# Down projection's tile 6 done whole, one norm beside half a tile, norm factors read in PSUM, weight splits moved

## The chip, the cores and the metric

The kernel runs on one core of a Trainium2 chip. A core has TensorE (PE) for matrix products, VectorE (DVE), ScalarE (ACT) and GpSimd (POOL) for the rest, and SyncE (SP), whose queue here issues the loads and stores. The metric is the device time of one execution in microseconds. Lower is better.

## The reference, cut to what matters

One layer of a hybrid block over 512 tokens of width 1024, in float32: a half-step SwiGLU FFN, a token mixer (gated DeltaNet beside latent attention) and a second half-step FFN. Each of the three works on a modulated RMS norm of x:

```python
def _modulate(x, shift, scale):
    return _rms(x) * (1.0 + scale[:, None, :]) + shift[:, None, :]
h = _modulate(x, sh1, s1)
x = x + 0.5 * g1[:, None, :] * _swiglu(h, ffn1_w_in[l], ffn1_w_out[l])
h = _modulate(x, sh2, s2)
y = _hybrid_mixer(h, ...)          # proj = h @ w_in, ..., mixed @ w_out
x = x + g2[:, None, :] * y
h = _modulate(x, sh3, s3)
x = x + 0.5 * g3[:, None, :] * _swiglu(h, ffn2_w_in[l], ffn2_w_out[l])
```

The norm needs the sum of squares over all 1024 channels of a token, so it can't be finished before the last channel tile of x is.

## The kernel before, in words

The activations lie transposed: x is eight tiles `xT[t]` of 128 channels by 512 tokens. Every float32 product is three matmuls (`mm3`, lines 259 to 261): the high parts `wh` x `xh`, then `wh` x `xl`, then `wl` x `xh`. A weight unit is 128 columns of a weight matrix, up to 8 x 128 x 128; SP loads it raw (`wr`), ACT casts the high part (`wh`, L191), DVE subtracts for the low part (`wl`, L192). Each of `wr`, `wh` and `wl` has four buffers, so a unit's cast waits until PE has read the unit four before it for the last time. `plan_units` fixes the order of the units, `prefetch` and `next_unit` say where in the code each is loaded and split.

FFN1's down projection (`down` with `norm`) makes the eight tiles of x: tiles 0 to 5 in one piece of 512 columns, three weight units each (`KPARTS`: 8, 8 and 6 of the 22 k-steps), then tile 6's first 256 tokens, tile 7's first, tile 7's second and tile 6's second; tile 6's units are loaded and split twice for this. When a tile is finished, DVE adds it to x (`finish`, L652), ACT squares it (L468), and POOL (first half of the tokens) or DVE (the rest) adds the squares into `na` (L470). This lets the norm of the first 256 tokens run beside the two last half tiles. `norm_half` is that norm: two matmuls sum the squares over the channels (`colsum`, L506), DVE takes mean and eps (`ve`, L512), POOL the power -1/2 (`ry`, L177), DVE makes two diagonal matrices of it (`dg`, L426), a matmul with ones spreads them over the partitions (`spread_diag`, L434), ACT copies the result from PSUM (`rb`, L436), and `modulate` makes of each tile of x a scaled one on DVE (`hm`, L452), the high part of h on ACT (`hh`, L454) and the low part on DVE (`hl`, L446). It is a generator: it runs on by a piece wherever `next(na)` stands.

The mixer begins with `latents`: `first_units` multiplies three weight units with the first 256 tokens of h, then with the second 256. It goes k by k over the three units; after places 5, 11 and 15 (`marks`) it runs a piece of the second half's norm, so the column sum L506 stands after six (k, unit) steps and L434 after twelve. Each unit has an accumulator of a pool of three PSUM banks (`acc`), given out in turn; the third unit's is the bank of the down projection's last half tile. `aux` is a pool of five banks for all else. The mixer's end has the same form: `out_half` makes eight half tiles of 256 tokens, twice, with the first half's norm between the tiles of the second, and FFN2 begins with `first_units`. There `prefetch` in `out_half` places the splits of FFN2's first units.

PE's order is held as the code has it (`matmuls_in_order`); ACT and DVE each take their instructions in the order that the scheduler wrote, one after the other.

## Time and profile before

| | |
|---|---|
| median of three runs | 1085.63 us (1085.16, 1085.63, 1088.35) |
| the profiled execution | 1088.02 us, of it 1086.2 us from the first to the last instruction |
| PE busy | 1056.7 us (97%) |
| DVE, ACT, POOL busy | 575.6, 390.6, 43.6 us |
| mean granted clock of PE | 0.991 |

A busy PE is one with a matmul under way; matmuls overlap, so their durations add up to more than the time that they take, and the pace is read from the starts. Idle time of another engine matters only where PE waits for it.

### The profile page before, as it was taken

How to read it: one execution, taken by the hardware profiler on the slowest of the kernel's cores; microseconds unless marked ns; L12 is line 12 of the kernel's file. 1: busy time of each engine (PE TensorE's matmuls, PEld its weight loads, DVE VectorE, ACT ScalarE, POOL GpSimd, SP SyncE). 2: the span in 40 equal slices, each digit the busy share in tenths (PEclk: the TensorE clock that was granted, in tenths of full speed). 3: DMA queues.
4: the chain of work that ended last, by engine and by line, in shares of the span. 5: the costliest groups of instructions: out<-in, count | busy, mean ns of one | idle time of the engine just before them, and what ended most of it. 6: DMA issues, size and time to landing. Idle time of an engine off the chain costs nothing.

```text
span 1086.2 us, 14130 instructions
## 1 busy us (share of the span) xinstructions
PE 1056.7 (97%) x5583; PEld 883.9 (81%) x5583; DVE 575.6 (53%) x1026; ACT 390.6 (36%) x644; POOL 43.6 (4%) x94
## 2 busy tenths in 40 slices
PE   6999999999999999998999999989999999999998
PEld 5788878788887899887887778988888888888887
DVE  4488984333587455469978546674333333322220
ACT  3342222222222345475584544344222222222220
POOL 1000000000000010102000031300000000000000
PEclk8999999999999999999999989999999999999999
DMA  9989973333697345211222001124333333333320
GB/s 275 270 244 297 288 219 97 95 95 92 205 290 239 109 124 165 74 39 46 71 70 72 21 1 39 40 78 118 98 97 97 97 97 97 91 102 111 97 73 30
DMA packets 210576, 132.04 MB, mean 122 GB/s; under 512 B 13633, under 2 KB 194638, under 8 KB 210510
## 3 DMA queue, kind: packets, MB, share of 16 engines
q1 hardware_dynamic: 210510, 131.14, 41.4%
q8 instruction: 44, 0.72, 0.3%
q14 instruction: 22, 0.18, 0.1%
HBM read 128.63 MB, written 2.49 MB: 121 GB/s over the span
## 4 chain that ended last, share of the span: by engine, by line
PE 86%; DVE 8%; DMA 2%; ACT 2%; issue 2%; SPq 1%; POOL 0%; DVEq 0%; POOLq 0%
PE pa L259 25%; PE pa L260 25%; PE pa L261 25%; DVE wl L192 1%; PE pb L407 1%; DMA ar<-in_w_ada 1%; PE pb L259 1%; PE pb L260 1%; PE pb L261 1%; PE pb L1144 1%; PE pb L1545 1%; DVE cv L1088 1%; DVE hl L446 0%; PE pb L1528 0%; POOL ry L177 0%
## 5 line engine op out<-in xcount | busy, mean ns | idle before, releaser
L191 ACT CAST wh<-wr 128x1024 fp32r<-128x1024 f32 (+1 forms) x170 | 173.7, 1023 | 504.4 <-PE pa L260 344.6
L259 PE MATMUL pa<-hh,wh 128*128 128x512 f32 (+1 forms) x885 | 340.0, 384 | 4.8 <-DVE xT L1731 2.7
L260 PE MATMUL pa<-hl,wh 128*128 128x512 f32 (+1 forms) x885 | 336.1, 380 | 0.0
L261 PE MATMUL pa<-hh,wl 128*128 128x512 f32 (+1 forms) x885 | 335.9, 380 | 0.0
L192 DVE TENSOR_TENSOR wl<-wr,wh 128x1024 fp32r<-128x1024 f32 (+1 forms) x170 | 201.6, 1187 | 236.3 <-ACT wh L191 230.8
L259 PEld LDWEIGHTS pa<-hh,wh 128*128 128x128 f32 x885 | 167.4, 189 | 39.5 <-issue 3.1
L261 PEld LDWEIGHTS pa<-hh,wl 128*128 128x128 f32 x885 | 167.4, 189 | 31.4 <-DVE wl L192 0.4
L260 PEld LDWEIGHTS pa<-hl,wh 128*128 128x128 f32 x885 | 167.5, 189 | 29.2 <-DVE hl L446 0.2
L259 PE MATMUL pa<-ah,wh 128*128 128x512 f32 (+1 forms) x418 | 150.1, 359 | 0.0
L261 PE MATMUL pa<-ah,wl 128*128 128x512 f32 (+1 forms) x418 | 148.8, 356 | 0.0
L260 PE MATMUL pa<-al,wh 128*128 128x512 f32 (+1 forms) x418 | 148.6, 356 | 0.0
L259 PEld LDWEIGHTS pa<-ah,wh 128*128 128x128 f32 x418 | 79.0, 189 | 12.6 <-ACT wh L191 1.7
L261 PEld LDWEIGHTS pa<-ah,wl 128*128 128x128 f32 x418 | 79.0, 189 | 11.4
L260 PEld LDWEIGHTS pa<-al,wh 128*128 128x128 f32 x418 | 79.0, 189 | 11.0
L590 DVE TENSOR_TENSOR af<-sg,pa 128x512 f32<-128x512 f32 x40 | 27.5, 687 | 103.3 <-PE pa L261 102.6
L544 DVE SCALAR_TENSOR_TENSOR aa<-ar,sc,aa 128x512 f32<-128x512 f32 x98 | 73.2, 751 | 14.2 <-DMA ar<-in_w_ada 12.5
L652 DVE SCALAR_TENSOR_TENSOR xT<-pa,mod,xT 128x512 f32<-128x512 f32 (+1 forms) x19 | 12.7, 667 | 49.1 <-PE pa L261 49.0
L592 ACT CAST ah<-af 128x512 fp32r<-128x512 f32 x44 | 27.5, 624 | 16.0 <-DVE af L590 16.0
L259 PE MATMUL pa<-mh,wh 128*128 128x256 f32 (+1 forms) x96 | 32.5, 341 | 0.2 <-ACT mh L1572 0.2
L260 PE MATMUL pa<-ml,wh 128*128 128x256 f32 (+1 forms) x96 | 31.3, 326 | 0.0
L261 PE MATMUL pa<-mh,wl 128*128 128x256 f32 (+1 forms) x96 | 31.2, 325 | 0.0
L593 DVE TENSOR_TENSOR al<-af,ah 128x512 fp32r<-128x512 f32 x44 | 30.2, 687 | 0.8 <-ACT ah L592 0.7
(355 smaller groups left out, 1008.8 us busy)
## 6 DMA issues: line engine op xcount, KB each, us to landing
wr<-in_ffn_w_in SPq DMA_DIRECT2D x82, 512.0 KB, 3.9
ar<-in_w_ada SPq DMA_DIRECT2D x48, 512.0 KB, 6.0
wr<-in_ffn_w_out SPq DMA_DIRECT2D x34, 512.0 KB, 4.3
ar<-in_w_ada SPq DMA_DIRECT2D x48, 256.0 KB, 5.1
wr<-in_w_in SPq DMA_DIRECT2D x21, 512.0 KB, 3.9
wr<-in_ffn_w_out SPq DMA_DIRECT2D x17, 384.0 KB, 4.7
wr<-in_w_out SPq DMA_DIRECT2D x8, 512.0 KB, 4.8
wr<-in_ffn_w_in SPq DMA_DIRECT2D x8, 384.0 KB, 7.5
```

Source lines behind the costliest of these rows:

```text
L191: self.nc.scalar.copy(hi, raw)
L192: self.nc.vector.tensor_tensor(out=lo, in0=raw, in1=hi.bitcast(F32), op=ALU.subtract)
L259: mm(out, wh, xh, start=start, stop=False)
L260: mm(out, wh, xl, start=False, stop=False)
L261: mm(out, wl, xh, start=False, stop=stop)
L407: nc.tensor.matmul(pg[32 * q:32 * q + 32, :256], self.sc[:, kc:kc + 1].to_broadcast([P, 32]), a[:, kc], start=(e == 0), stop=(e == 1), til ...
L544: nc.vector.scalar_tensor_tensor(out=acc, in0=a, scalar=sc, in1=acc, op0=ALU.mult, op1=ALU.add)
L590: nc.vector.tensor_tensor(out=a, in0=s, in1=pu, op=ALU.mult)
L592: nc.scalar.copy(ah, a)
L593: nc.vector.tensor_tensor(out=al, in0=a, in1=ah.bitcast(F32), op=ALU.subtract)
L652: nc.vector.scalar_tensor_tensor(out=self.xT[t][:, ts], in0=p[:, ts], scalar=gate[:, t:t + 1], in1=self.xT[t][:, ts], op0=ALU.mult, op1=AL ...
L1088: nc.vector.scalar_tensor_tensor(out=a[:, d:], in0=p[:, :NT - d], scalar=wj(3 - d), in1=a[:, d:], op0=ALU.mult, op1=ALU.add)
```

## The change: tile 6 whole, the norm in tile 7's second half, spread factors in PSUM, splits placed later

In `down`, tile 6 is done in one piece like tiles 0 to 5, and its second set of units goes from the plan. Tile 7 is done in halves; the first of the mixer's units is prefetched in its first half, the two next in its second, which is cut into pieces of two k-steps so that the norm's column sum stands after six k-steps and its spread after fourteen. `spread_diag` returns the PSUM bank itself, which `modulate` then reads; only phase 0 still copies it. `first_units` takes a lag for each unit: in the latents the third unit runs two k-steps behind the others. In `out_half` the prefetch of FFN2's units stands behind the update of x of tiles 3, 5 and 7 instead of before the matmuls of tiles 2, 4 and 6.

```diff
--- before.py
+++ after.py
@@ -233,7 +233,7 @@
                 for k0, n in KPARTS:
                     self.specs.append(lambda k0=k0, n=n, t=t: self.unit(w2[k0 * P:(k0 + n) * P, t * P:(t + 1) * P], n))
 
-        ffn(ins["ffn1_w_in"][0], ins["ffn1_w_out"][0], 3, [*range(KT), KT - 2])
+        ffn(ins["ffn1_w_in"][0], ins["ffn1_w_out"][0], 3, range(KT))
         w = ins["w_in"][0]
         for c in (2056, 2184, 2312, 2440, 2568):
             cols(w, c)
@@ -365,7 +365,8 @@
             if kt == 0:
                 for j in range(6):
                     nc.tensor.matmul(pu[j], hi[:, j, :], xh, start=True, stop=False)
-                rb = self.spread_diag(dg, NB)
+                rb = self.slot(s="rb")
+                nc.scalar.copy(rb, self.spread_diag(dg, NB))
             for j in range(6):
                 if j == 0 and more:
                     cols = self.phase0_cols(kt + 1, loads[kt + 1][0])
@@ -432,9 +433,7 @@
         nc = self.nc
         pr = self.aux()
         nc.tensor.matmul(pr[:, :n * P], self.ones, dg[:, :n * P], start=True, stop=True)
-        rb = self.slot(s="rb")
-        nc.scalar.copy(rb[:, :n * P], pr[:, :n * P])
-        return rb
+        return pr
 
     def modulate(self, kts, ts, rb, scale, shift):
 
@@ -479,12 +478,13 @@
             self.modulate(range(k, k + 2), ts, rb, self.mod[j + 1], self.mod[j])
             yield
 
-    def first_units(self, n, nb, lead, marks):
-
-
+    def first_units(self, lag, nb, marks):
+
+
+        n = len(lag)
         units = [self.next_unit(ahead=0) for _ in range(n)]
         ps = [self.acc() for _ in range(n)]
-        first = [(kt, i) for kt in range(KT) for i in range(lead)] + [(kt, i) for i in range(lead, n) for kt in range(KT)]
+        first = [(kt - lag[i], i) for kt in range(KT + max(lag)) for i in range(n) if 0 <= kt - lag[i] < KT]
         with self.matmuls_in_order(self.last_mm):
             for half in range(2):
                 ts = slice(half * HALF, half * HALF + HALF)
@@ -654,18 +654,16 @@
             if norm:
                 self.square_in(t, ts, accum)
 
-        def parts(t, ts, units=None, fine=False):
+        def parts(t, ts, units=None, by=8):
             p = self.acc()
             for i, (k0, n) in enumerate(KPARTS):
                 u = units[i] if units else self.next_unit()
-                if fine:
-                    self.dense(p, u, act, ts, 0, 4, FT - 1, k0)
+                for k in range(0, n, by):
+                    self.dense(p, u, act, ts, k, min(k + by, n), FT - 1, k0)
                     yield
-                self.dense(p, u, act, ts, 4 if fine else 0, n, FT - 1, k0)
-                yield
             finish(t, ts, p)
 
-        last = KT - 2 if norm else KT - 1
+        last = KT - 1
         side = Side()
         if norm:
             side.add(self.ada_rest((2, 3), True))
@@ -677,31 +675,28 @@
                 if not norm and i == 1 and t > 0:
                     self.store(t - 1, range(NB))
         side.flush()
+        units = [self.next_unit(ahead=0) for _ in KPARTS]
         if not norm:
-            t = KT - 1
-            units = [self.next_unit(ahead=0) for _ in KPARTS]
-            for i, _ in enumerate(parts(t, ha, units)):
+            for i, _ in enumerate(parts(last, ha, units)):
                 if i == 1:
-                    self.store(t - 1, range(NB))
-            for i, _ in enumerate(parts(t, hb, units)):
+                    self.store(last - 1, range(NB))
+            for i, _ in enumerate(parts(last, hb, units)):
                 if i == 1:
-                    self.store(t, range(2))
-            self.store(t, range(2, 4))
+                    self.store(last, range(2))
+            self.store(last, range(2, 4))
             return None
-        drain(parts(last, ha))
-        units = [self.next_unit(ahead=0) for _ in KPARTS]
         with self.matmuls_in_order():
-            drain(parts(last + 1, ha, units))
+            for i, _ in enumerate(parts(last, ha, units)):
+                if i == 1:
+                    self.prefetch(1)
             self.new_h()
             na = self.norm_half(0, accum, norm)
-            for i, _ in enumerate(parts(last + 1, hb, units, True)):
-                if i in (1, 3, 4):
+            for i, _ in enumerate(parts(last, hb, units, 2)):
+                if i in (2, 6, 8, 10):
                     next(na, None)
-                if i % 2:
-                    self.prefetch(i // 2 + 1)
-            for i, _ in enumerate(parts(last, hb)):
-                drain(na)
-                self.prefetch(3)
+                if i in (4, 8):
+                    self.prefetch(i // 4 + 1)
+            drain(na)
         return self.norm_half(1, accum, norm)
 
     def store(self, t, blocks):
@@ -717,7 +712,7 @@
 
     def ffn2(self, nb):
         act = []
-        ps = self.first_units(3, nb, 3, (5, 11, 15))
+        ps = self.first_units((0, 0, 0), nb, (5, 11, 15))
         act.append(self.glu(ps[0], ps[1]))
         act.append(self.glu(ps[2], self.proj(self.aux())))
         for f in range(2, FT):
@@ -896,7 +891,7 @@
         wkv = self.up_weight("mla_w_ukv", self.vcol["mla_kv_norm_w"], 2, 512)
         next(wq)
         next(wkv)
-        ps = self.first_units(3, nb, 3, (5, 11, 15))
+        ps = self.first_units((0, 0, 2), nb, (5, 11, 15))
 
         def gather(ps):
             parts, acc = [], None
@@ -1723,14 +1718,14 @@
         for t in range(KT):
             if half == 0 and t % 2 == 0:
                 self.wide.append(self.next_unit(ahead=1 if t < 6 else 0))
-            if half == 1 and t > 0 and t % 2 == 0:
-                self.prefetch(t // 2)
             p = self.acc()
             self.dense(p, self.wide[t // 2][t % 2], self.mixed, ts, k1=4, last=3)
             yield
             nc.vector.scalar_tensor_tensor(out=self.xT[t][:, ts], in0=p[:, ts], scalar=self.mod[5][:, t:t + 1],
                                            in1=self.xT[t][:, ts], op0=ALU.mult, op1=ALU.add)
             self.square_in(t, ts, accum)
+            if half == 1 and t > 1 and t % 2:
+                self.prefetch(t // 2)
             if na and t in (1, 2, 5):
                 next(na, None)
```

The next rows are DVE's at the end of FFN1's down projection, before, from the last but one scaled tile of the first 256 tokens to the mean of the second half's sum. `xT` is x, `hm` the scaled tile, `hh` and `hl` the parts of h, `wl` a weight unit's low part, `na` the sums of squares.

```order
L452 SCALAR_TENSOR_TENSOR hm_3323<-xT_106,mod_1791,rb_3238 128x256
L652 SCALAR_TENSOR_TENSOR xT_106<-pa_3290,mod_1297,xT_106 128x256
L452 SCALAR_TENSOR_TENSOR hm_3326<-xT_106,mod_1791,rb_3238 128x256
L192 TENSOR_TENSOR wl_3538<-wr_3536,wh_3537 128x1024
L446 SCALAR_TENSOR_TENSOR hl_3168<-hm_3323,mod_1297,hh_3167 128x256
L446 SCALAR_TENSOR_TENSOR hl_3170<-hm_3326,mod_1297,hh_3169 128x256
L470 TENSOR_TENSOR na_2257<-na_2257,sq_3392 128x256
L512 TENSOR_SCALAR ve_3439<-pb_3436 128x2
```

All eight tiles of the first half are modulated before the sum of the second half's squares into `na`. Now the same stretch, from the third tile on:

```order
L451 SCALAR_TENSOR_TENSOR hm_3258<-xT_106,mod_1791,pb_3236 128x256
L652 SCALAR_TENSOR_TENSOR xT_106<-pa_3177,mod_1297,xT_106 128x256
L451 SCALAR_TENSOR_TENSOR hm_3261<-xT_106,mod_1791,pb_3236 128x256
L192 TENSOR_TENSOR wl_3445<-wr_3443,wh_3444 128x1024
L445 SCALAR_TENSOR_TENSOR hl_3166<-hm_3258,mod_1297,hh_3165 128x256
L445 SCALAR_TENSOR_TENSOR hl_3168<-hm_3261,mod_1297,hh_3167 128x256
L451 SCALAR_TENSOR_TENSOR hm_3284<-xT_106,mod_1791,pb_3236 128x256
L451 SCALAR_TENSOR_TENSOR hm_3287<-xT_106,mod_1791,pb_3236 128x256
L445 SCALAR_TENSOR_TENSOR hl_3170<-hm_3284,mod_1297,hh_3169 128x256
L445 SCALAR_TENSOR_TENSOR hl_3172<-hm_3287,mod_1297,hh_3171 128x256
L451 SCALAR_TENSOR_TENSOR hm_3296<-xT_106,mod_1791,pb_3236 128x256
L469 TENSOR_TENSOR na_2257<-na_2257,sq_3293 128x256
```

The update of x (L652) stands in the third tile's place, and the sum (L469) behind the low part of a weight unit and most of the modulation of the tiles three to seven.

PE's, in the first units of the latents, before, around the column sum (L506); `pa` are the three units' accumulators:

```order
L259 MATMUL pa_3416<-hh_3157,wh_3362 128x256
L260 MATMUL pa_3416<-hl_3158,wh_3362 128x256
L261 MATMUL pa_3416<-hh_3157,wl_3363 128x256
L259 MATMUL pa_3417<-hh_3157,wh_3386 128x256
L260 MATMUL pa_3417<-hl_3158,wh_3386 128x256
L261 MATMUL pa_3417<-hh_3157,wl_3387 128x256
L506 MATMUL pb_3436<-ones_97,na_2257 128x1 x2
L259 MATMUL pa_3415<-hh_3159,wh_3332 128x256
```

Six (k, unit) steps stand before the sum, the last with the third unit. Now:

```order
L259 MATMUL pa_3324<-hh_3165,wh_3134 128x256
L260 MATMUL pa_3324<-hl_3166,wh_3134 128x256
L261 MATMUL pa_3324<-hh_3165,wl_3135 128x256
L259 MATMUL pa_3325<-hh_3165,wh_3219 128x256
L260 MATMUL pa_3325<-hl_3166,wh_3219 128x256
L261 MATMUL pa_3325<-hh_3165,wl_3220 128x256
L506 MATMUL pb_3345<-ones_97,na_2257 128x1 x2
L259 MATMUL pa_3326<-hh_3161,wh_3267 128x256
```

Still six steps before it, but of the first two units alone, so that they read the third tile of h (`hh_3165`, `hl_3166`); the third unit begins behind the sum.

DVE's at the end of the mixer's out projection, before, from the update of tile 6 to that of tile 7:

```order
L1731 SCALAR_TENSOR_TENSOR xT_106<-pa_6506,mod_1791,xT_106 128x256
L470 TENSOR_TENSOR na_5536<-na_5536,sq_6449 128x256
L452 SCALAR_TENSOR_TENSOR hm_6492<-xT_106,mod_2754,rb_6425 128x256
L470 TENSOR_TENSOR na_5536<-na_5536,sq_6472 128x256
L452 SCALAR_TENSOR_TENSOR hm_6495<-xT_106,mod_2754,rb_6425 128x256
L470 TENSOR_TENSOR na_5536<-na_5536,sq_6489 128x256
L446 SCALAR_TENSOR_TENSOR hl_6347<-hm_6492,mod_2754,hh_6346 128x256
L446 SCALAR_TENSOR_TENSOR hl_6349<-hm_6495,mod_2754,hh_6348 128x256
L1731 SCALAR_TENSOR_TENSOR xT_106<-pa_6523,mod_1791,xT_106 128x256
```

Now, from the update of tile 6 on:

```order
L1724 SCALAR_TENSOR_TENSOR xT_106<-pa_6405,mod_1791,xT_106 128x256
L469 TENSOR_TENSOR na_5443<-na_5443,sq_6388 128x256
L451 SCALAR_TENSOR_TENSOR hm_6400<-xT_106,mod_2754,pb_6324 128x256
L1724 SCALAR_TENSOR_TENSOR xT_106<-pa_6422,mod_1791,xT_106 128x256
L445 SCALAR_TENSOR_TENSOR hl_6254<-hm_6397,mod_2754,hh_6253 128x256
L445 SCALAR_TENSOR_TENSOR hl_6256<-hm_6400,mod_2754,hh_6255 128x256
L192 TENSOR_TENSOR wl_6441<-wr_6439,wh_6440 128x1024
L469 TENSOR_TENSOR na_5443<-na_5443,sq_6419 128x256
L451 SCALAR_TENSOR_TENSOR hm_6445<-xT_106,mod_2754,pb_6324 128x256
L469 TENSOR_TENSOR na_5443<-na_5443,sq_6436 128x256
L451 SCALAR_TENSOR_TENSOR hm_6448<-xT_106,mod_2754,pb_6324 128x256
L512 TENSOR_SCALAR ve_6485<-pb_6482 128x2
```

The update of tile 7 stands three rows behind that of tile 6 instead of eight; the low part of FFN2's third unit, which stood before the update of tile 6, stands behind it.

## Rows read from the trace of the kernel before

**Rows 1.** The page's part 4, the chain that ended last, by engine
```profile
PE 86%; DVE 8%; DMA 2%; ACT 2%; issue 2%; SPq 1%; POOL 0%; DVEq 0%; POOLq 0%
```

**Rows 2.** Timeline of PE, first norm: start us, us, instruction, [idle before]
```profile
353.68 0.39 PE L261 MATMUL pa<-ah,wl 128*128 128x512 f32 x1
...
356.40 0.39 PE L261 MATMUL pa<-ah,wl 128*128 128x512 f32 x1
...
378.57 0.28 PE L259 MATMUL pa<-ah,wh 128*128 128x256 f32 x1
...
386.49 0.28 PE L259 MATMUL pa<-ah,wh 128*128 128x256 f32 x1
...
389.37 0.50 PE L506 MATMUL pb<-ones,na 128*128 128x1 f32 x4
...
403.19 0.28 PE L259 MATMUL pa<-hh,wh 128*128 128x256 f32 x1
...
405.38 0.36 PE L259 MATMUL pa<-hh,wh 128*128 128x256 f32 x1 [1.31 <-ACT hh L454]
...
408.03 0.58 PE L506 MATMUL pb<-ones,na 128*128 128x1 f32 x4 [0.99 <-DVE na L470]
...
410.70 0.60 PE L434 MATMUL pb<-dg,ones 128*128 128x256 f32 x2
```

**Rows 3.** Chain in order of time before the first norm's second sum
```profile
404.44 0.40 DVE hm L452
...
405.62 1.14 DVE wl L192
...
407.55 0.35 DVE na L470
```

**Rows 4.** Groups by line and shape: xcount | busy us, mean ns | idle before
```profile
L191 ACT CAST wh<-wr 128x1024 fp32r<-128x1024 f32 x146 | 153.6, 1054 | 434.4 <-PE pa L260 274.6 <-issue 148.3 <-PE pa L261 4.1
...
L454 ACT ACTIVATE hh<-hm,mod 128x256 fp32r<-128x256 f32 x32 | 15.6, 509 | 9.6 <-DVE hm L452 9.6
L452 DVE SCALAR_TENSOR_TENSOR hm<-xT,mod,rb 128x256 f32<-128x256 f32 x32 | 14.9, 484 | 3.0 <-ACT rb L436 3.0
...
L652 DVE SCALAR_TENSOR_TENSOR xT<-pa,mod,xT 128x256 f32<-128x256 f32 x6 | 2.9, 485 | 21.4 <-PE pa L261 21.3
```

**Rows 5.** Timeline of POOL, first norm
```profile
387.77 0.74 POOL L470 TENSOR_TENSOR na<-na,sq 128x256 f32<-128x256 f32 x1 [6.17 <-ACT sq L468]
```

**Rows 6.** Timeline of ACT, first norm
```profile
389.50 1.05 ACT L191 CAST wh<-wr 128x1024 fp32r<-128x1024 f32 x1 [1.87 <-PE pa L260]
...
411.34 0.37 ACT L436 COPY rb<-pb 128x256 f32<-128x256 f32 x1 [4.86 <-PE pb L434]
```

**Rows 7.** Timeline of PE, second norm
```profile
711.33 0.28 PE L259 MATMUL pa<-hh,wh 128*128 128x256 f32 x1
...
715.23 0.58 PE L259 MATMUL pa<-hh,wh 128*128 128x256 f32 x1 [2.37 <-DVE xT L1731]
...
717.95 0.58 PE L506 MATMUL pb<-ones,na 128*128 128x1 f32 x4
...
721.02 0.67 PE L434 MATMUL pb<-dg,ones 128*128 128x256 f32 x2 [0.23 <-DVE dg L426]
```

**Rows 8.** Stretches of the second norm: us, busy by engine, PEclk, DMA share, GB/s
```profile
714.50:715.00 0.50, 0.00 (x0) 0.00 (x0) 0.50 (x2) 0.00 (x0) 0.00 (x0) 0.69 0.00 0
...
718.00:718.50 0.50, 0.50 (x6) 0.50 (x6) 0.50 (x3) 0.00 (x0) 0.00 (x0) 0.90 0.00 0
```

**Rows 9.** Timeline of DVE, second norm
```profile
705.77 0.48 DVE L1731 SCALAR_TENSOR_TENSOR xT<-pa,mod,xT 128x256 f32<-128x256 f32 x1 [0.35 <-PE pa L261]
...
714.68 0.49 DVE L1731 SCALAR_TENSOR_TENSOR xT<-pa,mod,xT 128x256 f32<-128x256 f32 x1
...
720.39 0.48 DVE L426 TENSOR_SCALAR dg<-ident,ry 128x128 f32<-128x128 f32 x2
```

**Rows 10.** Timeline of DVE, first norm
```profile
389.91 0.16 DVE L512 TENSOR_SCALAR ve<-pb 128x2 f32<-128x2 f32 x1 [2.74 <-PE pb L506]
```

## The prediction

> **What bounds the kernel now.** I read the chain that ended last first: TensorE (PE) holds 86% of it and VectorE (DVE) 8% [rows 1]. So time is won or lost only where PE stands still. The change touches two such places, and I call them the norms: the first, where FFN1's down projection hands over to the mixer's latents, and the second, where the mixer's out projection hands over to FFN2. Each squares and sums the new x, spreads 1/rms with a matmul (L434), and modulates eight tiles twice, by halves of 256 tokens.
>
> At the first norm the timeline of PE shows the half tiles running at 0.12 us a matmul, then in the first units of the latents two waits, 1.31 and 0.99 us [rows 2]. The second ends when DVE has added the last squares. The first is put down to ACT, but the matmul after it is the first to write the third unit's bank, and that bank comes free with DVE's update of x just before; so both are DVE being late. The chain of waits says the same: before the column sum (L506) stand only DVE steps, at 0.40 us for a modulating step, 1.14 for the low part of a weight split, 0.35 for a sum [rows 3]. These paces are less than the durations because DVE overlaps the start of one instruction with the end of the one before; I use paces inside a row of DVE work and durations for what waits on it.
>
> **The change part by part.** Sums are against the profiled execution itself (span 1086.2, run time 1088.02); the three runs have a median of 1085.63, so I add the difference to that.
>
> *Tile 6 whole.* A 512-column matmul takes 2.72/12 = 0.227 us, a 256-column one (386.49 - 378.57)/66 = 0.120 [rows 2]. Two halves cost 0.240, so 66 pairs merged save 66 x 0.0133 = 0.88 us. [...] The three reloads of tile 6's weights go too: three loads on SP's queue, three casts on ACT and three low parts on DVE, at most 1.05 and 1.14 us each [rows 3, 4]. Nothing ended late on them but through DVE having more to do, which the walk below counts. A POOL sum turns into a DVE one of 512 columns beside tile 7's first half, before DVE has any part of the norm to do: nothing.
>
> *The norm beside half a tile.* From the first sum to the end of the down projection PE had two half tiles of cover; now it has one. I walk it through on the old trace's clock. Tile 6 starts where it did and takes 66 x (0.227 - 0.120) = 7.04 us longer, so tile 7's first half starts at 385.61 instead of 378.57 and its second at 393.53. POOL's sum ended 2.02 us after that point [rows 2, 5], now at 395.55; the new L506 stands 18 matmuls in, at 395.69: no wait. In the old order 132 matmuls and two inserted ones (L506, L434) took 403.19 - 386.49 = 16.70 us, so the inserted ones cost 0.86; the half tile now ends at 393.53 + 7.92 + 0.86 = 402.31, 0.88 earlier. L434 stands some 24 matmuls and 0.45 us after L506, at 399.02.
>
> Now DVE and ACT. There are four buffers for split weights, and without the reloads the mixer's second, third and fourth weight unit take those of tile 7's units, which its second half is still reading. A cast starts 0.13 us after the matmuls that hold its buffer [rows 2, 6]: at 397.0, at 400.6 (behind a modulating step) and at 402.4, 1.05 us each [rows 4]. L434's output is ready 0.64 us after its start, when its ACT copy began [rows 2, 6], so DVE modulates from 399.66. In program order DVE does: two scale steps to 400.5, a low step at 400.7 (it waits for ACT's 0.51 [rows 4]), the third unit's low part 401.7 to 402.8, low step, scale, update of x (403.6), scale, the fourth unit's low part 404.4 to 405.5, two low steps to 406.3, two scales, two lows (407.4 to 408.2 with the wait for ACT), scale, and only then the sum, 408.6 to 409.0. L506 follows 0.13 later [rows 2, 3]: 409.15. PE, free at 402.31, has 18 matmuls before L506 (2.16 us), so it stands still some 4.7 us: about 1.6 of it for the low half of the third tile (ready 406.0) and 2.3 for the sum. From this L506 to the next L434 the order holds the same work, 2.67 us [rows 2], and that L434 didn't wait before: 411.82 against 410.70. **First norm: +1.1 us**. The bound below: if DVE were never late, L506 would stand at 404.47 instead of 408.03, a gain of 3.6.
>
> *The clock.* At the second norm PE stood idle 2.37 us, and the granted clock fell within that wait (0.69 mean over 714.5 to 715.0, then 0.50) and was back by 718.5 [rows 7, 8]. Twelve matmuls took 2.72 us there instead of about 1.6: 1.1 us. The waits of 1.31 and 0.99 at the first norm left the pace at 0.12 [rows 2]. After the change the first norm has a 2.3 us wait behind a stretch that is already half idle, nearer to the wait that lost the clock. I count the fall, at the 1.1 that it cost there and 0.1 for L506 itself: **+1.2 us** (bounds 0 and 1.3).
>
> *Norm factors read in PSUM.* Four ACT copies of 0.37 us go [rows 6]. In the first halves DVE wasn't waiting for them (a weight's low part stood between), in the second halves it was, but PE has 36 matmuls of other work after L434: nothing. In return 32 scale steps read one operand from PSUM. The nearest row is the update of x, same operation and shape with one operand in PSUM: 485 ns against 484 [rows 4]. I take 0; bounds 1 ns a step either way. The trace has no step with exactly this pair of operands. [...] The PSUM bank is held longer; the five aux banks have room for two sums, two spreads and the next projection.
>
> *Third unit behind by two (mixer), splits later (FFN2).* The lag is in the walk: the bank wait of 1.31 goes, and the low half of the third tile is late in its place. At the second norm I walk from DVE's update of tile 3 at 705.77 [rows 9]. The first scale step now follows at once (706.17), one sum waits for its square until 707.04, and the second unit's low part moves from before the updates of tiles 4 to 7 to behind tile 5. Update of tile 6 comes at 711.56, of tile 7 at 712.69 against 714.68 [rows 9]; PE's out projection was long done (711.33 [rows 7]). So the third unit's bank is free 2 us earlier, but its low part now stands behind the update, 713.89 to 715.12, and its third matmul waits for that: 715.17. Ten matmuls later, and behind the last sum (716.18), L506 stands at 716.45 against 717.95 [rows 7]: 1.5 earlier. But then the next L434 waits for DVE: the row after the sums is reached at 717.07 (L506 + 0.54, by 389.91 [rows 10] over 389.37), and behind it still stand two scales, four lows and a weight's low part (6 x 0.40 + 1.14, and 0.3 for ACT's step), so the diagonals run from 720.95 to 721.43 and L434 starts at 721.6; it started at 721.02, 0.15 after diagonals ready at 720.87 [rows 7, 9]. DVE is the bound there in both, and it gained nothing. **Second norm: +0.55 us.** Bounds: -1.5 if L434 follows PE, +1.5 if the 1.5 us wait before the third unit's low part drops the clock again, since L506 then comes 0.95 later (ten matmuls at the pace of 715.23 to 717.95) and DVE waits for it.
>
> Sum: 1.1 + 1.2 + 0.55 = +2.85 us: 1085.63 + 2.85 = **1088.5** (1090.9 for the profiled execution).
>
> **The rivals.** *Slower: the clock falls at the second norm too.* Place: the wait before the third unit's low part. For it: the clock fell there before. Against: that wait is 1.5 us, not 2.37. It decides when the granted clock is near 0.5 as the last low part lands at 715; price 0.95 on top, 1.1 + 1.2 + 1.5 = +3.8: 1089.4. *No fall at either:* 1.1 + 0.55 = +1.65: 1087.3; for it speak the waits of 1.31 and 0.99 without a fall. *Faster: half a tile is cover enough.* If ACT and DVE, three splits lighter, reach the sums on time, the first norm gives -3.6 and the second -1.5: 1080.5. Against it: the splits taken out are not those that stood before the sum, and buffers that the half tile holds push the new ones into its end. *PSUM reads slower:* 15 scale steps before the two decisive points; to pass the bound of no change they need 30 ns each; the rows show 1.
>
> **How the numbers follow.** Forecast 0.47, clock falls twice 0.25, no fall 0.17, faster 0.08, PSUM 0.03. A measurement of this kernel can't tell less than about 0.3%, 3.3 us, from no change. The forecast and no fall lie within that, the forecast by only 0.4, so part of it (0.04) is counted as slower: slower 0.32, same 0.60, faster 0.08. The range must hold no fall, the forecast and both falls with the scatter of the runs (1085.16 to 1088.35): 1084.6 to 1090.6. The forecast alone would have 1087 to 1090.
>
> **What would show it.** Right: in the first units of the latents a wait of over 1.4 us at the low half of the third tile and one of about 2.3 before L506, each behind a DVE weight split; a granted clock near 0.5 after it; the second norm's L506 earlier by about 1.5 us but its second L434 waiting for the diagonals; the scale steps at 484 ns. Wrong: a second L434 of the first norm earlier than at 410.7, or a second norm whose L434 doesn't wait.

## The result: slower by 0.47%

The changed kernel takes 1090.38 us (median of 15 runs, 1086.26 to 1092.89) against 1084.87 (1081.98 to 1088.35) for the kernel before on the same chip: ratio 1.0047, 95% interval 1.0032 to 1.0063, some 5 us. That lies in the forecast's range, 0.2 us under its upper end of 1090.6, and above its time of 1088.5; slower had been given 0.32, and 0.60 had gone to a difference too small to tell from none. The profiled execution took 1092.88 us (span 1091.1), mean granted clock 0.986 against 0.991.

### The profile after, at the first norm

The timeline of PE in the changed kernel, against [rows 2] (L435 is the spread matmul, L434 before):

```profile
395.62 0.50 PE L506 MATMUL pb<-ones,na 128*128 128x1 f32 x4
...
398.94 0.59 PE L435 MATMUL pb<-dg,ones 128*128 128x256 f32 x2
...
402.24 0.28 PE L259 MATMUL pa<-hh,wh 128*128 128x256 f32 x1
...
405.94 0.38 PE L260 MATMUL pa<-hl,wh 128*128 128x256 f32 x1 [1.39 <-DVE hl L445]
...
409.01 0.98 PE L506 MATMUL pb<-ones,na 128*128 128x1 f32 x4 [2.21 <-DVE na L469]
...
410.21 0.41 PE L260 MATMUL pa<-hl,wh 128*128 128x256 f32 x1
...
413.84 0.93 PE L435 MATMUL pb<-dg,ones 128*128 128x256 f32 x2
```

The first units begin at 402.24 where they began at 403.19. Then PE waits 1.39 us for the low half of the third tile and 2.21 for the last sum. From that sum to the spread matmul lie the same 18 matmuls as before, but they take 4.83 us (413.84 - 409.01) instead of 2.67: each 0.41 long instead of 0.28. The stretches say why (length in us; busy time of PE, of its weight loads, of DVE, ACT and POOL; PEclk, the granted clock as a share of full speed; DMA share; GB/s):

```profile
406.00:407.00 1.00, 0.80 (x5) 0.59 (x5) 1.00 (x3) 0.29 (x1) 0.00 (x0) 1.00 0.39 45
407.00:408.00 1.00, 0.00 (x0) 0.00 (x0) 0.81 (x3) 0.93 (x3) 0.00 (x0) 0.84 0.98 281
408.00:409.00 1.00, 0.00 (x0) 0.02 (x1) 1.00 (x4) 0.43 (x1) 0.00 (x0) 0.50 1.14 343
409.00:414.00 5.00, 4.99 (x23) 5.00 (x24) 1.68 (x6) 0.58 (x2) 0.87 (x1) 0.50 1.04 358
414.00:415.00 1.00, 1.00 (x7) 0.88 (x6) 0.19 (x1) 0.00 (x0) 0.00 (x0) 0.74 0.66 252
```

PEclk is 0.50 from within the second wait until behind the spread matmul. DVE's timeline has what PE waited for, the fourth weight's low part at 404.28 among the steps before the sum at 408.45, beside [rows 3]:

```profile
401.57 1.23 DVE L192 TENSOR_TENSOR wl<-wr,wh 128x1024 fp32r<-128x1024 f32 x1 [0.45 <-ACT wh L191]
...
404.28 1.22 DVE L192 TENSOR_TENSOR wl<-wr,wh 128x1024 fp32r<-128x1024 f32 x1
...
408.45 0.42 DVE L469 TENSOR_TENSOR na<-na,sq 128x256 f32<-128x256 f32 x1
```

### The profile after, at the second norm

PE's timeline, against [rows 7] (here 3.4 us later from the start, by the first norm):

```profile
718.53 0.58 PE L261 MATMUL pa<-hh,wl 128*128 128x256 f32 x1 [1.36 <-DVE wl L192]
...
720.84 0.85 PE L506 MATMUL pb<-ones,na 128*128 128x1 f32 x4
...
726.19 0.67 PE L435 MATMUL pb<-dg,ones 128*128 128x256 f32 x2 [0.68 <-DVE dg L427]
```

and the clock there, against [rows 8]:

```profile
718.00:719.00 1.00, 0.47 (x2) 0.47 (x3) 1.00 (x3) 0.00 (x0) 0.00 (x0) 0.65 0.00 0
719.00:724.00 5.00, 5.00 (x25) 5.00 (x25) 3.21 (x8) 1.02 (x2) 0.87 (x1) 0.50 0.36 107
724.00:725.00 1.00, 1.00 (x7) 1.00 (x6) 0.82 (x3) 0.77 (x2) 0.00 (x0) 0.50 0.22 64
```

The third unit's low part is waited for, the clock falls in that wait, and the spread matmul still waits for DVE's diagonals behind it.

### Where the 5 us are

The run times of one kernel scatter by up to 10 us, so I compare stretches of the profiled executions. Each number is the difference of two starts in PE's timeline. *First norm*: from a landmark in FFN1 (the modulation's column matmul, L563, at 337.32 before and 337.21 after) to the norm's second spread matmul. *Second norm*: from its first column sum (701.49 and 704.90) to its second spread matmul. *Between*: from the one spread matmul to the other norm's first column sum. "Fall" says whether PEclk was at 0.50 for part of it. Each row of stretches is one execution; the ratio is that of all runs.

| kernel | first norm | fall | between | second norm | fall | ratio to before |
|---|---|---|---|---|---|---|
| before | 73.38 | no | 290.79 | 19.53 | yes | 1 |
| changed | 76.63 | yes | 291.06 | 21.29 | yes | 1.0047 |
| changed again (e10) | 76.63 | yes | 287.19 | 20.78 | yes | 1.0048 |
| e1_fill | 74.48 | no | 294.77 | 19.93 | behind it | 1.0048 |
| e7_fill_first | 74.49 | no | 289.89 | 20.90 | yes | 1.0034 |
| e2_old_out | 76.63 | yes | 291.38 | 19.41 | no | 1.0042 |
| e4_out | 73.20 | no | 286.95 | 20.48 | yes | 1.0014 |
| e3_psum | 73.21 | no | 288.83 | 19.41 | no | 1.0000 |
| e8_late_sum | 76.27 | yes | 290.67 | 20.41 | yes | 1.0020 |
| e5_sum_first | 73.31 | no | 286.71 | 19.12 | yes | 0.9992 |
| e6_diag_first | 71.46 | no | 287.64 | 18.82 | no | 0.9931 |
| the same again (e9) | 71.46 | no | 287.62 | 19.23 | yes | 0.9985 |

The first norm is 3.25 us longer, 0.31 follow while the clock comes back (from the spread matmul to the second masked sum 34.12 instead of 33.81), and the second is 1.76 longer: 5.3 in all. From the second norm's spread matmul to the last matmul both profiles take 361.42 us. The spans differ by 4.9 us; the other 0.4 are gains of 0.11 ahead of the landmark, 0.04 in the rest of the stretch between and 0.27 behind the last matmul.

### The profile page after: what moved, and what is told of

It reads as the page before. It is cut to its first block, busy times and chain, and to the rows that moved or that the text cites. A ratio compares the mean times of both kernels' runs of the same rounds, so it can differ in the third digit from the quotient of the medians.

```text
span 1091.1 us, 13970 instructions
## 1 busy us (share of the span) xinstructions
PE 1060.5 (97%) x5517; PEld 884.4 (81%) x5517; DVE 572.4 (52%) x1022; ACT 385.8 (35%) x636; POOL 42.3 (4%) x93
## 4 chain that ended last, share of the span: by engine, by line
PE 86%; DVE 8%; ACT 2%; issue 2%; DMA 2%; POOL 0%; SPq 0%; POOLq 0%; DVEq 0%
PE pa L259 25%; PE pa L261 25%; PE pa L260 25%; DVE wl L192 1%; PE pb L408 1%; PE pb L259 1%; PE pb L260 1%; PE pb L261 1%; DMA xt<-in_x 1%; DVE cv L1083 1%; DVE hl L445 0%; PE pb L1139 0%; PE pb L1540 0%; POOL ry L177 0%; ACT bd L1173 0%
## 5 line engine op out<-in xcount | busy, mean ns | idle before, releaser
L191 ACT CAST wh<-wr 128x1024 fp32r<-128x1024 f32 (+1 forms) x167 | 170.5, 1022 | 513.6 <-PE pa L260 360.8
L192 DVE TENSOR_TENSOR wl<-wr,wh 128x1024 fp32r<-128x1024 f32 (+1 forms) x167 | 198.0, 1186 | 243.8 <-ACT wh L191 238.0
L259 PE MATMUL pa<-ah,wh 128*128 128x512 f32 (+1 forms) x396 | 146.2, 369 | 0.0
L261 PE MATMUL pa<-ah,wl 128*128 128x512 f32 (+1 forms) x396 | 144.9, 366 | 0.0
L260 PE MATMUL pa<-al,wh 128*128 128x512 f32 (+1 forms) x396 | 144.8, 366 | 0.0
L259 PEld LDWEIGHTS pa<-ah,wh 128*128 128x128 f32 x396 | 74.7, 189 | 13.6 <-ACT wh L191 1.7
L261 PEld LDWEIGHTS pa<-ah,wl 128*128 128x128 f32 x396 | 74.7, 189 | 12.2
L260 PEld LDWEIGHTS pa<-al,wh 128*128 128x128 f32 x396 | 74.7, 189 | 11.8
L652 DVE SCALAR_TENSOR_TENSOR xT<-pa,mod,xT 128x512 f32<-128x512 f32 (+1 forms) x18 | 12.4, 691 | 50.9 <-PE pa L261 50.9
```

Source lines behind the costliest of these rows:

```text
L191: self.nc.scalar.copy(hi, raw)
L192: self.nc.vector.tensor_tensor(out=lo, in0=raw, in1=hi.bitcast(F32), op=ALU.subtract)
L259: mm(out, wh, xh, start=start, stop=False)
L260: mm(out, wh, xl, start=False, stop=False)
L261: mm(out, wl, xh, start=False, stop=stop)
L652: nc.vector.scalar_tensor_tensor(out=self.xT[t][:, ts], in0=p[:, ts], scalar=gate[:, t:t + 1], in1=self.xT[t][:, ts], op0=ALU.mult, op1=AL ...
```

## The experiments

My theory: DVE's late rows cost 1.1 us at the first norm and 0.55 at the second, as walked, and the rest is the clock that falls in the waits. Rivals: the waits alone make the loss; the second norm's loss comes from elsewhere (the first norm, the PSUM reads); half a tile is too short a cover in any order. e1, e2, e4 and e5 ran on one chip, e7, e8, e3 and e6 together afterwards on another, e9 and e10 last on a third. The comments in the diffs are added here.

**e1_fill: the waits filled.** The product of the added matmuls is read by nobody.

```diff
+    def fill(self, unit, ts, n):
+        if n:
+            p = self.aux()
+            for _ in range(n):
+                self.nc.tensor.matmul(p[:, ts], unit[0][:, 0, :], self.h[0][0][:, ts], start=True, stop=True)
...
-        ps = self.first_units((0, 0, 0), nb, (5, 11, 15))
+        ps = self.first_units((0, 0, 0), nb, (5, 11, 15), {1: 3, 2: 14, -11: 4})
...
-        ps = self.first_units((0, 0, 2), nb, (5, 11, 15))
+        ps = self.first_units((0, 0, 2), nb, (5, 11, 15), {4: 12, -5: 16})
```

> The changed kernel with 49 more matmuls of 256 columns, whose product nobody reads, placed where TensorE stood still at the two norms: 12 ahead of the low half of the mixer's third tile, 16 ahead of the column sum (L506), and 3, 14 and 4 ahead of the first, third and last waits of FFN2's first units. VectorE's work is the same, in the same order. Theory (the late VectorE costs +1.1 and +0.55 us, the rest is the granted clock falling behind the waits): the granted clock stays at 1.00 at both norms, the spread matmul (L435) of the first norm stands near 411.8 on the old trace's clock instead of 413.84, that of the second norm near +0.55, and the time is about 3.4 us under the changed kernel's, +1.7 over the kernel before. Rival (the waits themselves make the whole loss, the clock is only a sign of them): L435 stays at 413.8 and the time at +5 over the kernel before.

The first norm is as the theory has it: the clock held at 1.00, the stretch 2.15 us shorter than the changed kernel's. But the time is not: 1090.69 us, ratio 1.0048 (1.0025 to 1.0071). The stretch between the norms is 294.77, the longest of all. In it stands a DRAM round trip of the attention stage that landed late (DVE's timeline; its read was issued at 581.94 and used 3.98 us later, 3.07 in the changed kernel), and the clock fell behind it:

```profile
585.92 0.69 DVE L886 TENSOR_TENSOR t<-t,mk 128x512 f32<-128x512 f32 x1 [2.75 <-DMA t<-t_d]
```

```profile
588.00:596.00 8.00, 7.16 (x34) 6.41 (x33) 4.09 (x9) 1.02 (x3) 0.00 (x0) 0.61 0.20 66
```

So the run's time was the rival's, not the theory's +1.7, and e7 had to ask whether the late round trip and the fall were chance.

**e7_fill_first: only the first norm's waits filled.** As e1 without the first of its two tables (FFN2's `{1: 3, 2: 14, -11: 4}`).

> The changed kernel with the unread matmuls of the first fill at the first norm alone: 12 ahead of the low half of the mixer's third tile and 16 ahead of the column sum; the second norm is the changed kernel's. Theory (the fill's time was lost in the attention stage, 4.0 us between the masked sums and the second norm against the kernel before, by a late DRAM round trip and a fall of the clock there, and that was chance): the first norm's spread matmul stands some 12.8 us behind the first half's (14.9 after the change), the clock stays at 1.00 there, the stretch from the masked sums (ones,lsq) to the second norm takes 253 to 257.5 us as in the other five profiles, and the time is 1 to 2.5 us under the changed kernel's. Rival (matmuls put into the waits move the fall of the clock to a later place): the stretch up to the second norm takes some 261 us again and the time is the changed kernel's.

PE's timeline at the first norm, the fill at L485, the sum at L515:

```profile
405.26 0.38 PE L260 MATMUL pa<-hl,wh 128*128 128x256 f32 x1 [0.30 <-DVE hl L445]
...
405.95 2.08 PE L485 MATMUL pb<-hh,wh 128*128 128x256 f32 x16
408.33 0.58 PE L515 MATMUL pb<-ones,na 128*128 128x1 f32 x4 [0.30 <-DVE na L469]
...
411.00 0.60 PE L435 MATMUL pb<-dg,ones 128*128 128x256 f32 x2
```

```profile
405.00:410.00 5.00, 4.45 (x35) 4.28 (x36) 4.33 (x12) 2.23 (x5) 0.82 (x1) 1.00 0.89 277
```

The sum comes when DVE has it, as in the changed kernel, and 18 matmuls later stands the spread: 2.67 us (411.00 - 408.33), the clock at 1.00. So the price of the fall up to the spread matmul is 2.14 us (76.63 - 74.49), and 74.49 - 73.38 = 1.11 is the price of DVE alone.

But the late round trip was not e1's chance. It stands here too (DVE's timeline, then PE's),

```profile
588.83 0.69 DVE L886 TENSOR_TENSOR t<-t,mk 128x512 f32<-128x512 f32 x1 [2.92 <-DMA t<-t_d]
```

```profile
589.58 1.16 PE L1233 MATMUL pb<-t,at 128*128 128x128 f32 x8 [2.64 <-DVE t L886]
```

where PE in the changed kernel waited 0.25:

```profile
590.39 1.16 PE L1224 MATMUL pb<-t,at 128*128 128x128 f32 x8 [0.25 <-DVE t L877]
```

The read was issued at 584.65 and used 4.18 us later. In the ten profiles without inserted matmuls that took 2.95 to 3.48 us and PE waited 0.15 to 0.86; in e1 it waited 2.48. So this wait stands in both filled kernels and in no other, and it takes back about what the fill gains at the first norm; why it goes with the fill stays open. Only the fall behind it was e1's: here the clock held, and the stretch between the norms is 289.89 (256.12 from the masked sums), within what the other profiles have.

The run times show no gain: ratio 1.0034 (1.0012 to 1.0057), a median of 1091.96 us, 5.9 above the kernel before on this chip (6.7 in e1, 5.5 for the changed kernel). The profiled execution, 1088.45 us at a clock of 0.997, is one of the faster of 1085.75 to 1095.83 (clocks down to 0.987), so for the others the rival, a fall moved to a later place, is not excluded. What e1 and e7 show is the price of the fall at the first norm, not that filling makes the kernel faster.

**e8_late_sum: the kernel before with a longer wait.**

```diff
+        for _ in range(late):    # late = 3 for the first norm's last sum, else 0
+            nc.vector.scalar_tensor_tensor(out=sq[:, :w], in0=sq[:, :w], scalar=1.0, in1=sq[:, :w], op0=ALU.mult, op1=ALU.max)
```

> The kernel before with three more VectorE instructions (each writes a square over itself, unchanged) ahead of the last sum of the first norm, so that the column sum (L506) there comes 1.2 to 1.4 us later and TensorE's wait for it is some 2.3 us instead of 0.99; all else is in the order of before. Theory (a wait of that length behind the waits before it loses the clock): the granted clock is near 0.50 behind the column sum, the 18 matmuls and the inserted ones from it to the spread matmul take 4.5 to 5 us instead of 2.67, and the spread matmul is 3.2 to 3.7 us later than in the kernel before. Rival (the clock fell after the change for another reason, such as a half idle stretch before it or TensorE's third unit lagging): the clock stays at 1.00 and the spread matmul is 1.2 to 1.4 us later.

PE's timeline and the clock:

```profile
403.53 0.36 PE L259 MATMUL pa<-hh,wh 128*128 128x256 f32 x1 [1.30 <-ACT hh L454]
...
407.55 0.69 PE L508 MATMUL pb<-ones,na 128*128 128x1 f32 x4 [2.36 <-DVE na L472]
...
411.74 0.60 PE L434 MATMUL pb<-dg,ones 128*128 128x256 f32 x2
```

```profile
407.00:408.00 1.00, 0.45 (x4) 0.48 (x4) 0.41 (x1) 0.00 (x0) 0.00 (x0) 0.94 1.15 351
...
409.00:410.00 1.00, 1.00 (x7) 1.00 (x7) 0.48 (x2) 0.00 (x0) 0.22 (x1) 0.50 1.10 378
...
411.00:412.00 1.00, 1.00 (x10) 0.97 (x8) 0.00 (x0) 0.00 (x0) 0.00 (x0) 0.86 1.06 365
```

The wait of 0.99 became 2.36, the clock fell, and the spread matmul is 2.89 us later (76.27 - 73.38; I had 3.2 to 3.7) for 1.37 of waiting. So a longer wait is followed by a fall outside the changed order too, in this one execution; the price, 1.52, is lower than I expected (4.19 us from sum to spread, I had 4.5 to 5), since the clock was back before the spread matmul here and behind it after the change. In run times the loss is unclear: 1.0020 (0.9997 to 1.0042).

**e2_old_out and e4_out: the two norms apart.** e2 is the changed kernel with out_half's splits where they were; e4 is the kernel before with PSUM reads and the splits moved.

```diff
@@ e2, against the changed kernel (e4 is the reverse, on the kernel before)
+            if half == 1 and t > 0 and t % 2 == 0:
+                self.prefetch(t // 2)
             p = self.acc()
...
-            if half == 1 and t > 1 and t % 2:
-                self.prefetch(t // 2)
```

> The changed kernel with the weight splits of the mixer's out projection put back where they were (ahead of tiles 2, 4 and 6 of its second half), so that only the first norm and the reads of the norm factors in PSUM differ from the kernel before. Theory: the first norm's loss stays whole, +3.1 us at its spread matmul with the clock fall there, and the second norm is as before (its clock falls as it did before): +3.3 over the kernel before, 1.8 under the changed one. Rival (the second norm's loss is a consequence of the first, or of the PSUM reads): the second norm's spread matmul is still 1.8 us late against its own start, and the time stays at +5.

> The kernel before with the norm factors read in PSUM and with the splits of the mixer's out projection placed as in the change; the first norm's order is that of before. Theory: the second norm's column sum comes about 0.5 us earlier and its spread matmul, which waits for VectorE's diagonals, 0.55 us later than before if the clock is back in time, 1.8 us later if it falls as in the changed kernel: +0.6 to +1.8 over the kernel before. Rival (the column sum's place decides the time): 0.5 us faster than the kernel before.

In the stretches each loss stays at its place. e2 keeps the whole first norm (76.63) and nothing of the loss at the second (19.41); e4 keeps the old first norm (73.20) and loses 0.95 at the second with the clock low. So neither rival holds in the traces. The run times can't tell: e2's ratio, 1.0042 (1.0026 to 1.0057), is more than the 3.3 us expected and overlaps the changed kernel's, and e4's is 1.0014 (0.9994 to 1.0034). One row of e2 shows what I hadn't seen: with the splits where they were and the clock at 1.00 (712 to 724) the spread matmul still waits for DVE,

```profile
722.67 0.67 PE L435 MATMUL pb<-dg,ones 128*128 128x256 f32 x2 [1.42 <-DVE dg L427]
```

so the fall that [rows 8] show in the kernel before cost it little. The difference is 0.12 us (19.53 - 19.41), and it isn't the fall's alone, since the PSUM reads change DVE's order too (see e3). In the kernel before DVE took the mean of the sum without a wait for PE, in the middle of a row that runs from 706.73 to the diagonals with no wait of note:

```profile
718.85 0.17 DVE L512 TENSOR_SCALAR ve<-pb 128x2 f32<-128x2 f32 x1
```

Half pace was hidden under DVE there.

**e3_psum: only the PSUM reads.** The kernel before, with `spread_diag` returning the PSUM bank.

> The kernel before with only the norm factors read in PSUM (four ACT copies fewer). Theory: a scale step takes what it took (485 ns by the nearest row, 470 to 480 in the changed kernel's profile), both spread matmuls stand where they did, and the time is the kernel before's, within 0.5 us. [...]

Ratio 1.0000 (0.9978 to 1.0023). A scale step takes 475 ns, against 484 with the copy in SBUF [rows 4]:

```profile
L451 DVE SCALAR_TENSOR_TENSOR hm<-xT,mod,pb 128x256 f32<-128x256 f32 x32 | 14.9, 475 | 2.9 <-PE pb L435 2.9
```

Both spread matmuls stand within 0.2 us of where they did. But the second norm's column sum comes 1.23 us earlier (15.23 us behind the first sum, 16.46 in the kernel before): without the ACT copy DVE scales the first tile straight behind an update of x, PE's wait of 2.37 us [rows 7] becomes two,

```profile
710.28 0.39 PE L259 MATMUL pa<-hh,wh 128*128 128x256 f32 x1 [1.66 <-DVE xT L1730]
...
711.56 0.36 PE L259 MATMUL pa<-hh,wh 128*128 128x256 f32 x1 [0.66 <-DVE xT L1730]
...
713.06 0.50 PE L505 MATMUL pb<-ones,na 128*128 128x1 f32 x4
```

and the clock stays at 1.00 (707 to 719). DVE is the bound of the spread matmul (at 717.24, behind a wait of 1.43 us for the diagonals), so little of that is time.

**e5_sum_first: the last sum first on DVE.** The changed kernel with two orders forced.

```diff
+            self.ends = self.summed                 # the last square (ACT) and sum (DVE)
+            with self.behind():                     # modulation of tiles 4 to 7 behind them
                 drain(na)
...
+                    self.ends = {mybir.EngineType.DVE: self.diag_last}
+                    with self.behind():             # the fourth split behind the diagonals
                         self.prefetch(1)
```

> The changed kernel with two orders forced on VectorE: at the first norm the squares and sums of the last tile stand ahead of the modulation of tiles 4 to 7, and at both norms the low part of the fourth weight split stands behind the diagonals. Theory (the order on VectorE ahead of the sum makes the loss): TensorE's wait ahead of the first norm's column sum goes, the column sum stands near 405.9 and the spread matmul near 408.6 on the old trace's clock (410.70 before, 413.84 after the change), the granted clock stays at 1.00 there; at the second norm the spread matmul comes 0.6 us earlier than before, or 0.4 later if the clock falls: 1.7 to 2.7 us under the kernel before, some 7 under the changed one. Rival (half a tile's cover is too short whatever the order, since the modulation of tiles 4 to 7 is then late): the third tile's units wait longer, the clock falls as well, and the time stays within 1 us of the changed kernel's.

PE's timeline at the first norm:

```profile
406.16 0.58 PE L510 MATMUL pb<-ones,na 128*128 128x1 f32 x4 [0.24 <-DVE na L470]
...
410.77 0.67 PE L436 MATMUL pb<-dg,ones 128*128 128x256 f32 x2 [1.78 <-DVE dg L427]
```

Half right. The sum comes 3.1 us earlier than after the change (68.70 from the landmark, 71.80 there), PE's wait for it is 0.24, the clock holds (the matmuls behind the sum start 0.12 us apart, against 0.21 after the change). But the spread matmul gains only what brings it level with the kernel before (73.31): the modulation that I moved behind the sum now stands ahead of the diagonals. I had counted 408.6 for it without walking DVE on past the sum. Ratio 0.9992 (0.9978 to 1.0005), against 1.0047 for the changed kernel: with half a tile of cover as there, DVE's order alone takes the loss away, so the rival doesn't hold.

**e6_diag_first: diagonals first too.** The second half's column sum and diagonals go ahead of the first half's tiles 6 and 7.

```diff
-                drain(na)
-        return self.norm_half(1, accum, norm)
+                next(na)                            # tiles 4 and 5
+        return self.both_halves(na, self.norm_half(1, accum, norm))
+    def both_halves(self, na, nb):
+        next(nb)                                    # second sum and diagonals
+        self.ends = {mybir.EngineType.DVE: self.diag_last}
+        with self.behind():
+            drain(na)                               # tiles 6 and 7
+        self.diag_last = self.low_last
+        yield
+        yield from nb
```

> The version with the sum first, and one more order forced on VectorE at the first norm: the second half's diagonals stand ahead of the modulation of the first half's tiles 6 and 7, and the fourth weight split behind all of it. Theory (VectorE's row between sum and diagonals is the bound there: the spread matmul waited 1.78 us for them in the last version): the spread matmul stands near 408.8 on the scale on which it stood at 410.77 in that version, tiles 6 and 7 are still in time, and the time is 1.5 to 2 us under that version's and 2 to 3 under the kernel before. Rival (the late tiles 6 and 7, or the late fourth split, hold TensorE up next): the spread matmul comes earlier but a wait of 1 to 2 us stands behind it, and the time is that of the last version.

```profile
404.94 0.58 PE L511 MATMUL pb<-ones,na 128*128 128x1 f32 x4 [0.25 <-DVE na L471]
...
407.70 0.67 PE L436 MATMUL pb<-dg,ones 128*128 128x256 f32 x2
```

No wait before the spread matmul, none of note behind it (the stretch to the masked sums is 33.85), and the first norm is 1.92 us shorter than in the kernel before. The ratio was 0.9931 (0.9906 to 0.9957, 7 runs), nearly three times what the two norms show (1.92 + 0.71), so it had to run again.

**e9_diag_again and e10_after_again: the last version and the changed kernel side by side.**

> The version with the diagonals first once more, beside the changed kernel on the same chip. Theory (only the two norms differ from the kernel before: their stretches are 2.6 us shorter in its profile, and the rest of its first ratio is chance, since the clock falls elsewhere in some executions and not in others): 2 to 4 us under the kernel before. Rival (its runs keep the clock better throughout, with mean granted clocks of 0.998 where the kernel before has 0.987 to 0.998): 6 to 8 us under the kernel before again, with clocks of 0.997 to 1.000.

> The changed kernel again, for a second profile and for runs beside the last version's. Theory: its first norm's stretch (from the modulation's column sums of FFN1 to the second spread matmul) is 3.2 us longer than before's with the clock at 0.50 behind the second wait, as in its first profile; its second norm's is 0.9 to 1.8 us longer, by whether the clock falls there; 4 to 6 us over the kernel before and 6 to 9 over the last version. Rival (the fall at the first norm is one execution's chance): the first norm's stretch is 1.1 us longer, with the clock at 1.00.

e9: 0.9985 (0.9965 to 1.0004), 1.7 us under the kernel before, with clocks of 0.987 to 0.998 like the others. The two norms are 1.92 and 0.30 us shorter. So the rival doesn't hold. The two ratios of this one kernel lie outside each other's intervals. The 7 runs of e6 had clocks of 0.994 to 1.000, and I put most of the difference down to where the clock fell in them, which isn't shown. That the last version is faster than the kernel before rests on the traces (2.2 us at the two norms here) and on e6's runs; e9's alone don't show it, and the size stays open. e10: 1.0048 (1.0031 to 1.0065); the first norm's stretch is the same to 0.01 us as in the first profile, with the fall again. On this chip the last version is 0.63% faster than the changed kernel.

## Why the prediction held, and the step that was too small

The range held by 0.2 us, and with luck: it had been stretched to take in a fall at both norms, a branch with 0.25. The forecast alone had 1087 to 1090 and missed, and the 0.60 on a difference under 0.3% was misplaced (the interval begins at 1.0032).

*Tile 6 whole, and the walk on DVE: right.* The first column sum was forecast at 395.69 and stands at 395.62, the second half's end at 402.31 (402.24), the waits at 1.6 and 2.3 (1.39 and 2.21), the second sum at 409.15 (409.01). The forecast for DVE alone, +1.1, is e7's +1.11.

*The clock at the first norm: right that it falls, too small in size.* This is the step that failed: "I count the fall, at the 1.1 that it cost there and 0.1 for L506 itself: +1.2 us (bounds 0 and 1.3)". I took the price of a fall from the second norm of the kernel before, where 12 matmuls ran at half pace. After the change all 18 matmuls from sum to spread did, and some behind: 2.14 us (76.63 - 74.49) and another 0.31 (0.52 in e10) until the clock was back. From the rows, the clock was low for 0.32 + 6 + 0.52 = 6.8 us (a mean of 0.84 over one us is 0.32 us at half pace), against 0.31 + 3 + 0.1 = 3.4 at the old second norm, [rows 8] with the stretch between them,

```profile
715.00:718.00 3.00, 2.77 (x13) 2.78 (x14) 3.00 (x7) 1.44 (x3) 0.00 (x0) 0.50 0.00 0
```

and as much at e8's first norm. A single fall with its own length was no bound for another. e8 shows that at the very place from which I had taken the price: its second norm is the kernel before's, in the same order and behind the same wait (2.36 us), but the clock was low for 0.92 + 5 + 0.9 = 6.8 us, and the spread matmul came 0.88 us later than there (20.41 - 19.53):

```profile
715.00:716.00 1.00, 0.00 (x0) 0.00 (x0) 1.00 (x3) 0.41 (x2) 0.00 (x0) 0.54 0.12 37
716.00:721.00 5.00, 4.87 (x23) 4.87 (x24) 4.89 (x13) 2.41 (x5) 0.87 (x1) 0.50 0.18 47
721.00:722.00 1.00, 1.00 (x7) 1.00 (x7) 0.78 (x3) 0.00 (x0) 0.00 (x0) 0.55 0.94 285
```

Nor was 1.1 what the fall had cost the kernel before: e2 and e3 put that at 0.12 at most, as DVE hid it.

*The second norm: the times of the walk right, one cause and the branch wrong.* Its sum was to come 1.5 us earlier and its spread 0.55 later. With the clock held up to there (e1) they are 1.54 earlier (14.92 from the first sum instead of 16.46) and 0.40 later. But I had counted the 1.5 under the moved splits and the PSUM reads at nothing, and e3 has 1.23 of it from the PSUM reads alone. And the clock fell in the wait of 1.36 us, the rival that had 0.25; its price of 0.95 on top was measured as 0.55 (e4), 0.85 (e10), 0.97 (e7) and 1.36 (the first profile), each against e1. In the first profile the clock was low for 6.8 us there, in e4, e7 and e10 for 3.4, behind the same wait; in e10:

```profile
716.00:717.00 1.00, 0.90 (x6) 0.90 (x7) 1.00 (x4) 0.20 (x1) 0.00 (x0) 0.88 0.00 0
717.00:720.00 3.00, 3.00 (x16) 3.00 (x15) 1.72 (x5) 0.82 (x2) 0.87 (x1) 0.50 0.60 178
720.00:721.00 1.00, 1.00 (x10) 1.00 (x9) 1.00 (x3) 0.00 (x0) 0.00 (x0) 0.92 0.00 0
```

*PSUM reads: right in the time.* A scale step takes 474 ns in the changed kernel and 475 in e3 against 484 with the copy in SBUF, shorter by more than the 1 ns that I had as bounds; e3's time is unchanged.

In sum: 1.11 + 2.14 + 0.31 + 0.40 + 1.36 = 5.3 where 2.85 was forecast. Of the 2.5 missing, 1.25 are the size of the first fall (2.45 for 1.2) and 1.2 the second norm, where the fall came that I had not counted (1.76 for 0.55).

## What to carry to other kernels

Where an engine that feeds TensorE is late, walk it on to the last thing that TensorE needs, not only to the first: moving the sum ahead only won back the loss (73.31 us, 73.38 in the kernel before), and a gain came when the diagonals stood ahead too (71.46). A wait of TensorE can cost more than its length, through the clock (2.14 us more behind waits of 1.39 and 2.21 here), and that price differed with how long the clock stayed low (3.4 or 6.8 us here) and with how much work followed at half pace before something else was the bound, so it is to be read at the place itself. Where single run times scatter by 10 us, compare stretches between landmarks that both traces have, and look through the rest of both traces before the gain of a stretch is called time: what the fill won at the first norm was lost again at a round trip some 180 us later.

## What was unexpected of the hardware

The same order with the same waits doesn't always lose the clock. At the second norm, waits of 0.24, 0.59 and 1.36 us were followed by a fall in the first profile, e4, e7, e9 and e10 (a clock of 0.50 over 719 to 724, 0.72 over 710 to 716, 0.83 over 710 to 720 in e7 and in e9, 0.59 over 716 to 720; e5's clock fell there too, 0.57 over 712 to 716), and by none in e6, which is the same kernel as e9:

```profile
704.00:716.00 12.00, 8.68 (x66) 7.87 (x65) 11.37 (x28) 5.17 (x13) 0.87 (x1) 1.00 0.31 89
```

With the splits where they were and the factors read in PSUM (e2 and e3, waits of 1.66 and 0.66) it stayed at 1.00, while in the kernel before and in e8 a wait of 2.37 and 2.36 was followed by a fall to 0.50. Elsewhere in the mixer, where no kernel here differs, falls came in some profiles and not in others, and with them the stretch between the norms changes: 287.19 us in e10 without a fall (1.00 from 420 to 710) and 286.71 in e5, the shortest; 290.79 and 291.06 with two in the kernel before and the first profile (0.83 over 500 to 510 in both, 0.66 over 640 to 650 in the one, 0.83 over 640 to 660 in the other), 294.77 in e1 with the late round trip and the fall behind it (0.61 over 588 to 596). That is a large part of the scatter of the run times, as far as one profile of each can tell.
